# A hybrid pooling / state-space decoder step: another order for the first group of the scan

## The chip, the core and the metric

The kernel runs on one NeuronCore of a Trainium2 chip, in fp32. Five engines work from queues of their own, each strictly in order: TensorE (PE, matmuls and transposes into PSUM), VectorE (DVE), ScalarE (ACT), GpSimd (POOL) and SyncE (SP, which issues nearly all DMA loads and stores here). An instruction that waits for another engine or for a DMA holds up everything behind it in its queue. The metric is the device time of one execution in microseconds (us).

## The reference

One decoder layer for 512 prompt tokens and 8 sample rows (one new token each, with cached state), 520 columns in all. What matters here is the input projection and branch B, the state-space scan, in 8 groups of 4 heads:

```python
proj = h @ w_in                                # u | z | xBC | dt | gates
xbc  = causal_conv(xbc, prev, conv_w, conv_b)  # 4 taps, then silu; sample rows use their cached taps
dt   = softplus(dt_raw + dt_bias);  dA = dt * -exp(A_log)
Acs  = cumsum(dA within a chunk of 128)
decay  = exp(where(mask, Acs[l] - Acs[s], -inf))
scores = einsum(C, B)[..., None] * decay
y_diag = einsum(scores, x * dt)
h_next = h * exp(Acs[-1]) + einsum(B, exp(Acs[-1] - Acs), x * dt)
y_off  = einsum(C, h, exp(Acs))
y = (y_diag + y_off + D * x) * silu(z)         # then norm, projection, merge, FFN
```

Sample rows take one step of the same recurrence from a cached state: `h' = h * exp(dA) + dt * x * B`, `y = C . h'`.

## The kernel before

Activations lie transposed, channels on the 128 partitions and the 520 tokens along the row. A **unit** is a weight block of 128 output channels by 1024 inputs (512 KB): loaded by SP into `raw`, split into a high and a low part (`whi`, cast on ACT, L116; `wlo`, subtraction on DVE, L117), and used by one **column**, 48 matmuls of L129 (three products for each of 8 input blocks, two halves) into one of two PSUM buffers `m` (or into two banks). PE's order is the program order, in this part also that of ACT, DVE, POOL and, from `sp_order(True)` on, of SP: what is emitted first stands first in its engine's queue. `ahead(n)` emits load and split of units before they are due; `perform` keeps two units ahead.

Each group g of the scan has four convolution columns, x0, x1 (2 x 128 channels of x), bb and cc (B and C), and z columns zz. `conv` (L626) copies the PSUM result to `xb` and, scaled by the last tap, to `v` (ACT, L638, L639), and adds the other three taps (DVE, L646). POOL clears the 3 columns ahead of `xb` (L634), keeps the new conv state (`cvp`, `cvs`, L640, L641) and adds `cpre`, the cached taps of the sample rows, to the last 8 columns of `v` (L642). `end`, put off to the next `flush`, does tanh (ACT, L652), the product that completes silu (DVE, L653) and a copy of the 8 sample columns (POOL, L654) to `xs_s` or `bc_s`. `cpre` itself is made once by five POOL operations from the cached states `cvs` (L599 loads them, L604 and L606 multiply and add).

Columns of group 0 for dt, x0 and x1 are computed in `start`, while the norm is finished; its bb and cc columns are the first behind it. `dt_parts` makes dt and `acs` (DVE, some 17 small operations in `dtmp`) and stores `acs` to DRAM (`dacs`) and the sample rows' dt (`dds`, `dscr`), which come back spread over the partitions as `dtx`. `dec_load` brings `acs` back as `dec`, each row spread over all partitions (1 MB for a group; that of group 1 goes to a part of `aa`); the first `dec` lies where `dtmp` lay. `tokens_dt` transposes dt and `acs` on PE (L614) to `tok` (L616) inside the x1 column of group 1.

The rest comes in generators whose steps are strewn between columns. `decays` (L671): four chunks, each exp (ACT, L684, not for chunk 0), four Relu (L687) and exp (L688). `scan`: transposes of x and B (L717, L727), C.B (L734), masked to `cbm` (DVE, L736), chunk states (PE, L756), the chain of states `hst` (copy on ACT, L759; then three times a POOL product L761 and a DVE addition L763), `scores` (DVE, L742: `dec` times `cbm`), `decayed` (DVE, L695: `ce` times C) and two y (PE, L778, L780). `sample`, stepped by `part`: transpose of `bc_s` (PE, L806), a store and two loads (L809, L794, L795), the POOL product L799 and a DVE sum L803. For group 0 these steps stand among the columns of group 1.

Of the kernel before, what the change touches and what calls it, by code (L numbers as in the profile page):

```python
# [52 lines left out]
def tile_decoder(ctx: ExitStack, tc: tile.TileContext, I: dict, O: dict):  # L53
# [381 lines left out]
    def start():  # L435
# [88 lines left out]
        rest(4)  # L524
        ahead(2)
        for k in range(5, KD):
# [62 lines left out]
    def ssd_open(*_):  # L589
        G["yp_"], G["yp"] = opened("yp")  # L590
        G["ab_"], ab = opened("ab")
        G["aa"] = ab.tile([P, KD, T], F32, name="aa")
        S["pool"], S["sp"] = opened("ssd")
        sp = S["sp"]
        S["dt"] = dt_parts(sp)
        next(S["dt"])

        cvs = S["cvs"] = sp.tile([P, 32, NS, 4], F32, name="cvs")
        nc.sync.dma_start(out=cvs, in_=I["sconv"])  # L599
        cpre = sp.tile([P, 32, NS], F32, name="cpre")  # L600
        ctmp = sp.tile([P, 32, NS], F32, tag="gz", name="ctmp", bufs=2)
        for k in range(3):
            w = cwh[:, 32 * k : 32 * k + 32].unsqueeze(2).broadcast_to([P, 32, NS])
            nc.gpsimd.tensor_tensor(ctmp if k else cpre, cvs[:, :, :, k], w, ALU.mult)  # L604
            if k:
                nc.gpsimd.tensor_tensor(cpre, cpre, ctmp, ALU.add)  # L606
        S.update(cpre=cpre)
# [18 lines left out]
    def conv(i, outs, dst, keep, mix=None):  # L626
# [8 lines left out]
        with urgent():  # L635
            for o, t0, t1 in outs:
                shape = halves if t1 - t0 == T else lambda ap: ap
                nc.scalar.copy(shape(xb[:, 3 + t0 : 3 + t1]), o)  # L638
                nc.scalar.activation(shape(v[:, t0:t1]), o, AF.Identity, bias=cwh[:, 128 + i : 129 + i], scale=w(3))  # L639
        nc.gpsimd.tensor_copy(cvp[:, i], xb[:, TP : TP + 3])  # L640
        nc.gpsimd.tensor_copy(S["cvs"][:, i, :, 3], xb[:, TP + 3 : TP + 11])  # L641
        nc.gpsimd.tensor_tensor(v[:, TP:T], v[:, TP:T], S["cpre"][:, i], ALU.add)  # L642
        if mix:
            next(mix)
        for k in range(3):
            nc.vector.scalar_tensor_tensor(v[:, 0:TP], xb[:, k : k + TP], w(k), v[:, 0:TP], ALU.mult, ALU.add)  # L646
            if mix:
                next(mix)
        flush()

        def end():
            nc.scalar.activation(t, v, AF.Tanh, bias=0.0, scale=1.0)  # L652
            nc.vector.scalar_tensor_tensor(dst, t, 1.0, v, ALU.add, ALU.mult)  # L653
            nc.gpsimd.tensor_copy(keep, dst[:, TP:T])  # L654
# [44 lines left out]
    def scan(g, xg, bt, ct):  # L699
# [6 lines left out]
        tok = S["tok"]  # L706
        dec = S.pop(("dec", g))

# [55 lines left out]
        hst += hn  # L764
        scores((2, 3) if g else range(4))
        if not g:
            decayed(g, ct)
        nc.sync.dma_start(out=O["ssmp"][:, 256 * g : 256 * g + 256], in_=hst[4].rearrange("p h d -> p (h d)"))
        yield

        for i in range(2):
# [158 lines left out]
    def zend(i):  # L930
        return lambda: gated(i, S.pop(f"gz{i}"))

    def dt_more():
        next(S["dt"])

    for g in range(NG):
        todo(x0(g), *([X0(g)] if g else []))
        if g > 1:
            todo(step(g - 1))
        if g:  # L940
            todo(part(g - 1))
        todo(x1(g), *([X1(g)] if g else []))
        if g == 0:
            todo(dt_more)
        elif g == 1:
            todo(decay(0, 2))
            todo(step(0))
            todo(step(0))
        else:
            todo(step(g - 1))  # L950
# [4 lines left out]
        else:  # L955
            if g == 1:
                todo(decay(0, 2))
                todo(step(0))
            todo(part(g - 1))
            todo(decay(g))  # L960
        todo(cc(g), CC(g))
        if g:
            todo(part(g - 1))
            todo(decay(g))
            todo(zz(2 * g - 2), ZZ(2 * g - 2))
            todo(step(g - 1))
            todo(zend(2 * g - 2))
            todo(part(g - 1))
# [7 lines left out]
        if g:  # L976
            todo(part(g))
        else:
            todo(flush)
            todo(part(0))  # L980

# [575 lines left out]
```

## Time and profile before

| what | us |
|---|---|
| time, median of 3 runs (lowest to highest) | 1131.33 (1130.84 to 1132.9) |
| time of the profiled execution | 1131.08 |
| its span, first to last instruction | 1129.1 |
| PE busy in the span | 1078.7 (96%) |
| DVE, ACT, POOL busy | 697.6, 465.1, 349.2 |
| PE busy in 0 to 56, norm and first products | 47.4 |
| PE busy in 56 to 140, opening of the scan | 58.2 of 84 |
| PE busy in 140 to 500 | 359.7 of 360 |

PE is nearly always busy, so the few stretches in which it isn't are what an edit of the order can win, and the profile of such a stretch has to be read by what ended each wait. In a row of the timeline stand the start, the duration, the engine, the line, what is written and read, the count, and in brackets the idle time of the engine before it with what ended it. A list of waits gives the waiting instruction, the one that ended its wait, and total, count and longest in us. A row of the view by stretches ends with the granted PE clock (1.00 is full), the DMA engines' busy share, and GB/s.

### The profile page before, as it was taken

The page shows a single profiled execution, that of the slowest core. Times are in us where ns is not written, and L with a number is a line of the kernel's source. Part 1 is how long each engine was busy: PE and PEld are TensorE (multiplying, and loading weights), DVE is VectorE, ACT ScalarE, POOL GpSimd, SP SyncE. Part 2 cuts the span into 40 slices and gives each one's busy share as a digit, 9 for nine tenths or more (in the row PEclk, how much of TensorE's full clock was granted, in tenths as well). Part 3 has the DMA queues.
Part 4 walks back from the last instruction along what each step waited for, and adds up shares of the span by engine and source line. Part 5 has one row for each costly group of instructions (what it writes and reads, how often), then busy time and mean ns, then how long its engine had stood idle before and what let it go on. Part 6 is the DMA issues. An engine that isn't in the chain of part 4 may idle for free.

```text
span 1129.1 us, 22192 instructions
## 1 busy us (share of the span) xinstructions
PE 1078.7 (96%) x9345; PEld 1050.5 (93%) x9345; DVE 697.6 (62%) x963; ACT 465.1 (41%) x774; POOL 349.2 (31%) x498
## 2 busy tenths in 40 slices
PE   7949699999999999999999999999999999999995
PEld 6839599999999999999999999899999999999995
DVE  5663677787787788788757745655656653323332
ACT  4244646646656544575433323542222222222320
POOL 1131324334344342100000000289999960000001
PEclk9979799999999999999999999999999999999998
DMA  9326346246345332454435427356676652323212
GB/s 364 119 96 157 112 129 187 94 144 175 101 147 186 115 123 99 152 166 157 145 131 169 161 90 255 112 178 206 216 211 204 206 162 94 89 85 103 85 52 76
DMA packets 58467, 165.34 MB, mean 146 GB/s; under 512 B 10880, under 2 KB 16512, under 8 KB 57600
## 3 DMA queue, kind: packets, MB, share of 16 engines
q1 hardware_dynamic: 51712, 142.96, 39.0%
q0 software_dynamic: 6656, 20.98, 6.4%
q8 instruction: 73, 1.20, 0.4%
q14 instruction: 26, 0.21, 0.1%
HBM read 151.05 MB, written 12.86 MB: 145 GB/s over the span
## 4 chain that ended last, share of the span: by engine, by line
PE 88%; DVE 4%; issue 2%; DMA 2%; ACT 2%; POOL 1%; SPq 0%; DVEq 0%; POOLq 0%; ACTq 0%
PE m L129 77%; PE b L129 4%; PE b L778 2%; DMA raw<-in_win 1%; PE b L756 1%; PE b L780 1%; PE b L301 1%; DVE v L646 1%; PE b L734 1%; PE b L207 1%; PE b L717 1%; DVE acc L391 0%; DMA xT<-in_xT 0%; DMA raw<-in_wada 0%; POOL xn L1219 0%
## 5 line engine op out<-in xcount | busy, mean ns | idle before, releaser
L129 PE MATMUL m<-hh,whi 128*128 128x260 f32 (+1 forms) x1840 | 382.0, 287 | 1.7 <-ACT hh L475 1.0
L129 PE MATMUL m<-hl,whi 128*128 128x260 f32 (+1 forms) x1840 | 375.2, 284 | 3.3 <-DVE hl L481 3.1
L129 PE MATMUL m<-hh,wlo 128*128 128x260 f32 (+1 forms) x1840 | 375.2, 284 | 0.0
L117 DVE TENSOR_TENSOR wlo<-raw,whi 128x1024 fp32r<-128x1024 f32 (+2 forms) x169 | 234.0, 1387 | 151.1 <-ACT whi L116 148.3
L116 ACT CAST whi<-raw 128x1024 fp32r<-128x1024 f32 (+2 forms) x169 | 173.1, 1027 | 357.4 <-PE m L129 240.2
L129 PEld LDWEIGHTS m<-hh,whi 128*128 128x128 f32 x1840 | 287.1, 190 | 8.0 <-issue 3.2
L129 PEld LDWEIGHTS m<-hl,whi 128*128 128x128 f32 x1840 | 286.3, 190 | 4.1 <-DVE hl L481 3.8
L129 PEld LDWEIGHTS m<-hh,wlo 128*128 128x128 f32 x1840 | 286.9, 190 | 0.0
L341 POOL TENSOR_TENSOR r<-me,mhalf 128x5 f32<-128x5 f32 (+2 forms) x6 | 6.4, 1065 | 439.9 <-DVE me L340 439.9
L646 DVE SCALAR_TENSOR_TENSOR v<-xb,cwh,v 128x512 f32<-128x512 f32 x96 | 72.9, 760 | 52.8 <-ACT v L639 30.2
L1323 DVE TENSOR_TENSOR fs<-m,fs 128x520 f32<-128x520 f32 (+2 forms) x23 | 15.4, 675 | 70.6 <-PE m L129 69.8
L638 ACT COPY xb<-m 128x520 f32<-128x520 f32 (+1 forms) x31 | 17.9, 577 | 93.4 <-PE m L129 93.4
L129 PE MATMUL m<-ah,whi 128*128 128x260 f32 x264 | 53.2, 283 | 0.0
L129 PE MATMUL m<-ah,wlo 128*128 128x260 f32 x264 | 53.1, 282 | 0.0
L129 PE MATMUL m<-al,whi 128*128 128x260 f32 x264 | 53.0, 282 | 0.0
L129 PE MATMUL m<-gh,whi 128*128 128x260 f32 x256 | 52.8, 288 | 0.0
L129 PE MATMUL m<-gl,whi 128*128 128x260 f32 x256 | 51.3, 282 | 0.0
L129 PE MATMUL m<-gh,wlo 128*128 128x260 f32 x256 | 51.3, 282 | 0.0
L1312 POOL TENSOR_TENSOR hs<-hs,ht 128x512 f32<-128x512 f32 x32 | 47.8, 1494 | 0.8
L799 POOL TENSOR_TENSOR h<-h,cc 128x1024 f32<-128x1024 f32 x16 | 38.3, 2395 | 25.2 <-DMA cc<-dbc 24.2
L1310 POOL TENSOR_TENSOR ht<-bb,xds 128x512 f32<-128x512 f32 x32 | 41.0, 1282 | 2.2 <-DMA bb<-dbc 1.7
L129 PEld LDWEIGHTS m<-gh,whi 128*128 128x128 f32 x256 | 39.2, 188 | 2.5 <-PE b L301 1.3
(300 smaller groups left out, 1747.3 us busy)
## 6 DMA issues: line engine op xcount, KB each, us to landing
raw<-in_win SPq DMA_DIRECT2D x73, 512.0 KB, 4.8
raw<-in_wfi SPq DMA_DIRECT2D x44, 512.0 KB, 4.4
araw<-in_wada SPq DMA_DIRECT2D x24, 512.0 KB, 4.2
h<-in_sssm SPq DMA_DIRECT2D x16, 512.0 KB, 4.1
raw<-in_wssd SPq DMA_DIRECT2D x16, 512.0 KB, 3.4
hs<-in_sssm POOLq DMA_DIRECT2D x32, 256.0 KB, 4.1
out_ssms<-hs POOLq DMA_DIRECT2D x32, 256.0 KB, 3.5
raw<-in_wfo SPq DMA_DIRECT2D x16, 512.0 KB, 3.5
```

Source lines behind the costliest of these rows:

```text
L116: nc.scalar.copy(hi, raw)
L117: nc.vector.tensor_tensor(lo, raw, hi.bitcast(F32), ALU.subtract)
L129: nc.tensor.matmul(o, a[:, k, c0 : c0 + P], b[:, t0:t1], start=f, stop=e)
L207: nc.tensor.matmul(ps[32 * i : 32 * i + 32, 0:n], sc[:, k], raw[:, n * i : n * i + n], start=first, stop=last)
L301: nc.tensor.matmul(ps[32 * i : 32 * i + 32, 0:256], scr[:, k], w[:, 256 * i : 256 * i + 256], start=k == 0 and j == 0, stop=k == KD - 1 an ...
L638: nc.scalar.copy(shape(xb[:, 3 + t0 : 3 + t1]), o)
L646: nc.vector.scalar_tensor_tensor(v[:, 0:TP], xb[:, k : k + TP], w(k), v[:, 0:TP], ALU.mult, ALU.add)
L778: nc.tensor.matmul(o, xdt[:, c, 2 * i + h], dec[:, c, 2 * i + h], start=c == 0, stop=False)
L799: nc.gpsimd.tensor_tensor(h0, h0, cc.unsqueeze(2).broadcast_to([P, 4, 2, P]), ALU.mult)
L1310: nc.gpsimd.tensor_tensor(t, bb.unsqueeze(2).broadcast_to([P, 2, 2, P]), at(xds), ALU.mult)
L1312: nc.gpsimd.tensor_tensor(h, h, t, ALU.add)
L1323: nc.vector.tensor_tensor(view(s[:, t0:t1]), u, view(s[:, t0:t1]), ALU.mult)
```

## The change

Six edits, all in the order of emission. (1) `ahead(3)`: a third unit (x0 of group 1) is loaded and split ahead of the end of `start`. (2) The making of `cpre` becomes `conv_state`, called in the x1 convolution of group 0 behind its taps instead of in `ssd_open`. (3) The three small POOL operations of `conv` (add of `cpre`, `cvp`, `cvs`) move from behind the ACT operations into `end`, ahead of tanh, for all 32 convolutions. (4) The decay chunks of group 0 (`decay(0)`) and the first of group 1 are emitted later, and the scores and `ce` products of group 0 one step later than the end of the state chain, with an added `yield`. (5) The first sample steps (`part(0)`) come later, the transpose of `bc_s` behind the x1 column of group 1, and the others follow. (6) `dec` of a group is kept in `S` rather than popped.

```diff
@@ -522,7 +522,7 @@
         rows(5, 6)
         products(4)
         rest(4)
-        ahead(2)
+        ahead(3)
         for k in range(5, KD):
             products(k)
         first["ps"] = outs
@@ -597,6 +597,10 @@
 
         cvs = S["cvs"] = sp.tile([P, 32, NS, 4], F32, name="cvs")
         nc.sync.dma_start(out=cvs, in_=I["sconv"])
+
+    def conv_state():
+
+        sp, cvs = S["sp"], S["cvs"]
         cpre = sp.tile([P, 32, NS], F32, name="cpre")
         ctmp = sp.tile([P, 32, NS], F32, tag="gz", name="ctmp", bufs=2)
         for k in range(3):
@@ -637,18 +641,20 @@
                 shape = halves if t1 - t0 == T else lambda ap: ap
                 nc.scalar.copy(shape(xb[:, 3 + t0 : 3 + t1]), o)
                 nc.scalar.activation(shape(v[:, t0:t1]), o, AF.Identity, bias=cwh[:, 128 + i : 129 + i], scale=w(3))
-        nc.gpsimd.tensor_copy(cvp[:, i], xb[:, TP : TP + 3])
-        nc.gpsimd.tensor_copy(S["cvs"][:, i, :, 3], xb[:, TP + 3 : TP + 11])
-        nc.gpsimd.tensor_tensor(v[:, TP:T], v[:, TP:T], S["cpre"][:, i], ALU.add)
         if mix:
             next(mix)
         for k in range(3):
             nc.vector.scalar_tensor_tensor(v[:, 0:TP], xb[:, k : k + TP], w(k), v[:, 0:TP], ALU.mult, ALU.add)
             if mix:
                 next(mix)
+        if i == 1:
+            conv_state()
         flush()
 
         def end():
+            nc.gpsimd.tensor_tensor(v[:, TP:T], v[:, TP:T], S["cpre"][:, i], ALU.add)
+            nc.gpsimd.tensor_copy(cvp[:, i], xb[:, TP : TP + 3])
+            nc.gpsimd.tensor_copy(S["cvs"][:, i, :, 3], xb[:, TP + 3 : TP + 11])
             nc.scalar.activation(t, v, AF.Tanh, bias=0.0, scale=1.0)
             nc.vector.scalar_tensor_tensor(dst, t, 1.0, v, ALU.add, ALU.mult)
             nc.gpsimd.tensor_copy(keep, dst[:, TP:T])
@@ -704,7 +710,7 @@
             decayed(g, ct)
         yield
         tok = S["tok"]
-        dec = S.pop(("dec", g))
+        dec = S["dec", g]
 
         xdt = sp.tile([P, 4, 4, 64], F32, tag="xdt", name=f"xdt{g}")
         xde = sp.tile([P, 4, 4, 64], F32, tag="xde", name=f"xde{g}")
@@ -762,11 +768,14 @@
             yield
             nc.vector.tensor_tensor(hn[c], hn[c], sv[c], ALU.add)
         hst += hn
-        scores((2, 3) if g else range(4))
-        if not g:
-            decayed(g, ct)
+        if g:
+            scores((2, 3))
         nc.sync.dma_start(out=O["ssmp"][:, 256 * g : 256 * g + 256], in_=hst[4].rearrange("p h d -> p (h d)"))
         yield
+        if not g:
+            scores(range(4))
+            decayed(g, ct)
+            yield
 
         for i in range(2):
             yb = bank()
@@ -930,6 +939,9 @@
     def zend(i):
         return lambda: gated(i, S.pop(f"gz{i}"))
 
+    def scores_first():
+        next(gens[0])
+
     def dt_more():
         next(S["dt"])
 
@@ -937,15 +949,17 @@
         todo(x0(g), *([X0(g)] if g else []))
         if g > 1:
             todo(step(g - 1))
-        if g:
+        if g == 2:
+            todo(part(0))
+        if g > 1:
             todo(part(g - 1))
         todo(x1(g), *([X1(g)] if g else []))
         if g == 0:
             todo(dt_more)
         elif g == 1:
-            todo(decay(0, 2))
             todo(step(0))
             todo(step(0))
+            todo(part(0))
         else:
             todo(step(g - 1))
         todo(bb(g), BB(g))
@@ -954,16 +968,22 @@
             todo(dt_more)
         else:
             if g == 1:
-                todo(decay(0, 2))
                 todo(step(0))
+                todo(decay(0, 3))
+            else:
+                todo(decay(g))
             todo(part(g - 1))
-            todo(decay(g))
         todo(cc(g), CC(g))
+        if g == 1:
+            todo(decay(0))
+            todo(scores_first)
         if g:
             todo(part(g - 1))
             todo(decay(g))
             todo(zz(2 * g - 2), ZZ(2 * g - 2))
             todo(step(g - 1))
+            if g == 1:
+                todo(decay(1))
             todo(zend(2 * g - 2))
             todo(part(g - 1))
             todo(decay(g))
@@ -977,7 +997,6 @@
             todo(part(g))
         else:
             todo(flush)
-            todo(part(0))
 
     todo(sp_order(False))
     todo(lambda: ordered.__exit__(None, None, None) and None)
```

**PE and POOL, opening.** PE's queue around the sample transpose, before: `m51` is the cc column of group 0, `m55` the x0 column of group 1.

```order
L129 MATMUL m51_800<-hl_102,whi42_564 128x260 x2
L129 MATMUL m51_800<-hh_101,wlo42_565 128x260 x2
L806 MATMUL b52_870<-cst_75,bc_s_91 16x128
L129 MATMUL m55_882<-hh_101,whi46_772 128x260 x2
L129 MATMUL m55_882<-hl_102,whi46_772 128x260 x2
```

PE's queue around the same transpose after the change (now L815): `m57` is the x1 column of group 1, `m65` its bb column.

```order
L129 MATMUL m57_941<-hh_101,wlo49_791 128x260 x2
L723 MATMUL b59_1014<-cst_75,xg0_652 128x128 x4
L723 MATMUL b60_1021<-cst_75,xg0_652 128x128 x4
L733 MATMUL b61_1028<-cst_75,bt0_705 128x128 x4
L815 MATMUL b62_1034<-cst_75,bc_s_91 16x128
L129 MATMUL m65_1046<-hh_101,whi52_870 128x260 x2
```

The transpose has gone behind two columns and the transposes of x and B. POOL's queue at the same place of the program, before:

```order
L604 TENSOR_TENSOR cpre_646<-cvs_644,cwh_96 128x256
L604 TENSOR_TENSOR ctmp_647<-cvs_644,cwh_96 128x256
L606 TENSOR_TENSOR cpre_646<-cpre_646,ctmp_647 128x256
L604 TENSOR_TENSOR ctmp_647<-cvs_644,cwh_96 128x256
L606 TENSOR_TENSOR cpre_646<-cpre_646,ctmp_647 128x256
L634 MEMSET xb0_654 128x3
L640 COPY cvp_89<-xb0_654 128x3
L641 COPY cvs_644<-xb0_654 128x8
L642 TENSOR_TENSOR v0_655<-v0_655,cpre_646 128x8
```

and POOL after the change:

```order
L638 MEMSET xb0_653 128x3
L638 MEMSET xb1_664 128x3
L608 TENSOR_TENSOR cpre_675<-cvs_650,cwh_96 128x256
L608 TENSOR_TENSOR ctmp_676<-cvs_650,cwh_96 128x256
L610 TENSOR_TENSOR cpre_675<-cpre_675,ctmp_676 128x256
L608 TENSOR_TENSOR ctmp_676<-cvs_650,cwh_96 128x256
L610 TENSOR_TENSOR cpre_675<-cpre_675,ctmp_676 128x256
L655 TENSOR_TENSOR v0_654<-v0_654,cpre_675 128x8
L656 COPY cvp_89<-xb0_653 128x3
```

The two memsets now stand ahead of the five operations, which are still ahead of everything else.

**SP, the loads of the opening.** SP's queue before, from the store of `acs` on (`raw50` is the cc unit of group 1, `raw54` and `raw57` its two z units, `aa` the decays of group 1):

```order
L575 DMA dacs_782<-acs_700 128x128
L581 DMA dscr_787<-dds_784 32x2x8
L585 DMA dtx_93<-dscr_787 64x16x8 x4
L107 DMA raw50_797<-in_win 128x1024
L668 DMA dec0_864<-dacs_782 128x4x512
L668 DMA aa_629<-dacs_782 128x4x512
L809 DMA dbc_97<-bcs0_872 16x128
L107 DMA raw54_879<-in_win 128x1024
L794 DMA h0_0_0_943<-in_sssm 128x1024
L795 DMA cc_0_0_944<-dbc_97 128x512
L107 DMA raw57_951<-in_win 128x1024
```

SP after the change (`raw53` and `raw56` are the z units now):

```order
L107 DMA raw50_794<-in_win 128x1024
L674 DMA dec0_861<-dacs_779 128x4x512
L674 DMA aa_635<-dacs_779 128x4x512
L107 DMA raw53_874<-in_win 128x1024
L107 DMA raw56_939<-in_win 128x1024
L818 DMA dbc_97<-bcs0_1036 16x128
L107 DMA raw64_1043<-in_win 128x1024
L803 DMA h0_0_0_1136<-in_sssm 128x1024
L804 DMA cc_0_0_1137<-dbc_97 128x512
```

The sample rows' store and loads have gone behind both z units and the next x0 unit.

**ACT and POOL, the state chain of group 0.** ACT's queue around the copy that opens the chain, before (`t17` is the tanh of group 1's bb; `aa` and `ce1` belong to the decays of group 1):

```order
L116 CAST whi67_1158<-raw57_951 128x1024
L638 COPY xb25_1214<-m69_1165 128x520
L639 ACTIVATE v25_1215<-m69_1165,cwh_96 128x520
L759 COPY hst0_0_1229<-b70_1223 128x256
L652 ACTIVATE t17_1117<-v17_1116 128x520
L684 ACTIVATE ce1_1152<-aa_629 128x512
```

ACT after the change; here the last three rows are the fourth decay chunk of group 0:

```order
L116 CAST whi67_1140<-raw56_939 128x1024
L642 COPY xb25_1196<-m69_1147 128x520
L643 ACTIVATE v25_1197<-m69_1147,cwh_96 128x520
L765 COPY hst0_0_1208<-b70_1202 128x256
L658 ACTIVATE t17_1097<-v17_1096 128x520
L690 ACTIVATE aa_635<-dec0_861 128x512
L693 ACTIVATE dec0_861<-dec0_861,tok_964 128x128 x4
L694 ACTIVATE dec0_861<-dec0_861 128x512
```

POOL's queue there, before:

```order
L640 COPY cvp_89<-xb17_1115 128x3
L641 COPY cvs_644<-xb17_1115 128x8
L642 TENSOR_TENSOR v17_1116<-v17_1116,cpre_646 128x8
L654 COPY xs_s_90<-xg1_881 128x8
L799 TENSOR_TENSOR h0_0_0_943<-h0_0_0_943,cc_0_0_944 128x1024
L634 MEMSET xb25_1214 128x3
L640 COPY cvp_89<-xb25_1214 128x3
L641 COPY cvs_644<-xb25_1214 128x8
L642 TENSOR_TENSOR v25_1215<-v25_1215,cpre_646 128x8
L761 TENSOR_TENSOR hst0_1_1230<-hst0_0_1229,cd0_1023 128x256
L761 TENSOR_TENSOR hst0_2_1231<-hst0_1_1230,cd0_1023 128x256
L761 TENSOR_TENSOR hst0_3_1232<-hst0_2_1231,cd0_1023 128x256
```

and after the change:

```order
L638 MEMSET xb25_1196 128x3
L767 TENSOR_TENSOR hst0_1_1209<-hst0_0_1208,cd0_1117 128x256
L767 TENSOR_TENSOR hst0_2_1210<-hst0_1_1209,cd0_1117 128x256
L767 TENSOR_TENSOR hst0_3_1211<-hst0_2_1210,cd0_1117 128x256
L655 TENSOR_TENSOR v17_1096<-v17_1096,cpre_675 128x8
L656 COPY cvp_89<-xb17_1095 128x3
L657 COPY cvs_650<-xb17_1095 128x8
L660 COPY bc_s_91<-bt1_1045 128x8
L808 TENSOR_TENSOR h0_0_0_1136<-h0_0_0_1136,cc_0_0_1137 128x1024
```

The add to `v17`, which its tanh needs, and the sample product have gone from ahead of the state chain to behind it; the `bt` copy stands between them.

## The prediction, as made before the result was known

> **What bounds the kernel now.** I read the list of what TensorE (PE) waited for first, then its timeline. From 60 to 140 us the list names two waits: the one in the first timeline row below (16.94 us, ended by POOL), and this one (total, times, longest). None of that size follows.
>
> ```profile
> PE b L778 <- DVE dec L742: 8.9, 1, 8.9
> ```
>
> ```profile
> 83.40 0.38 PE L806 MATMUL b<-cst,bc_s 128*16 128x128 f32 x1 [16.94 <-POOL xb L634]
> ...
> 98.73 0.49 PE L129 MATMUL m<-hh,whi 128*128 128x260 f32 x2
> ...
> 132.00 0.80 PE L129 MATMUL m<-hh,whi 128*128 128x260 f32 x2
> ```
>
> The first hole is the sample transpose L806: it stands in PE's queue ahead of the x0 column of group 1 and needs `bc_s`, the end of all four first convolutions. The second is y of group 0 (L778), which needs the masked decays. Three times matter below: the start of the first hole (83.40 less 16.94 is 66.46), the bb column of group 1 at 98.73, and the zz1 column behind both holes at 132.00. After 132.00 PE is the bound again, so **the change is worth what it moves that zz1 column**, as long as later groups do not lose it again.
>
> **The opening: sample rows' preparation later.** Before, the five `cpre` operations (L604, L606) stand in POOL's queue ahead of the memset of `xb`, and DVE's six convolution steps wait for them.
>
> ```profile
> 59.17 0.75 POOL L604 TENSOR_TENSOR cpre<-cvs,cwh 128x256 f32<-128x256 f32 x1 [18.21 <-issue]
> ```
> ```profile
> 63.15 4.58 DVE L646 SCALAR_TENSOR_TENSOR v<-xb,cwh,v 128x512 f32<-128x512 f32 x6 [5.90 <-POOL xb L634]
> ```
>
> Now the memset is first, so DVE may begin at about 59.2, when ScalarE (ACT) has written `v`, and 3.9 us seem won. But `cpre` starts at 59.17 all the same (it waits only for the load of `cvs`), and it must still end before tanh, since the add of `cpre` now stands ahead of it. What do the two engines do side by side?
>
> ```profile
> 122.87 0.61 POOL L761 TENSOR_TENSOR hst<-hst,cd 128x256 f32<-128x256 f32 x1
> 124.01 1.05 POOL L761 TENSOR_TENSOR hst<-hst,cd 128x256 f32<-128x256 f32 x1 [0.53 <-DVE hst L763]
> 125.60 1.05 POOL L761 TENSOR_TENSOR hst<-hst,cd 128x256 f32<-128x256 f32 x1 [0.53 <-DVE hst L763]
> ```
> ```profile
> 123.85 0.74 DVE L646 SCALAR_TENSOR_TENSOR v<-xb,cwh,v 128x512 f32<-128x512 f32 x1
> ```
>
> The same POOL operation takes 0.61 alone and 1.05 when it meets that DVE step; 123.85 + 0.74 + 0.61 = 125.2 against a real end of 125.06. They take turns. So six steps (4.58) and five `cpre` (3.9) need 8.5 us from 59.17 on: 67.7, where they ended before. Bounds: 0.7 later (all DVE first, then `cpre`, add and tanh) to 3.9 earlier (no turns); I take 0, by the row. [...]
>
> **Three units split ahead, transpose moved.** The third weight split leaves the middle of the opening: one cast on ACT and one subtraction (1.22) on DVE. Its place is now ahead of `dt`, where DVE stands idle for 3.3 us until PE has ended the first products and ACT has read them:
>
> ```profile
> 56.95 0.30 DVE L553 SCALAR_TENSOR_TENSOR dtmp<-dtmp 128x136 f32<-128x136 f32 x1 [3.34 <-ACT dtmp L552]
> ```
>
> So it costs nothing there; without that cover it would move `dt` and all behind it by up to the 1.2 us of this row:
>
> ```profile
> 76.98 1.22 DVE L117 TENSOR_TENSOR wlo<-raw,whi 128x1024 fp32r<-128x1024 f32 x1
> ```
> ```profile
> 77.10 0.78 ACT L639 ACTIVATE v<-m,cwh 128x520 f32<-128x520 f32 x1 [0.91 <-DVE xg L653]
> ```
>
> PE now runs the x0 column of group 1 from 66.5 to 72.2 (a column is 5.76, row below). The x1 column needs the PSUM buffer of the cc column, which that ACT row frees at 77.9. So the 16.9 us hole becomes one of **5.6**. PE restarts at half clock after it (0.50, third number from the end in the stretch 85:86 below), which costs some 2 us of the x1 column and nothing of the path, because of what comes next.
>
> ```profile
> 141.64 5.76 PE m L129 x48
> ```
>
> PE must then wait for the token copy. `tok` on ACT stands behind the split of the CC unit, whose 512 KB load is issued by SyncE (SP) behind four `dtx` loads:
>
> ```profile
> 83.87 1.08 SPq L107 DMA_DIRECT2D raw<-in_win  x1
> 93.86 0.38 SPq L668 DMA_DIRECT2D dec<-dacs  x1
> ...
> 97.03 1.61 SPq L794 DMA_DIRECT2D h<-in_sssm  x1
> ```
> ```profile
> 85.00:86.00 1.00, 1.00 (x7) 1.00 (x6) 0.95 (x1) 0.02 (x1) 0.00 (x0) 0.50 0.40 23
> ...
> 88.00:89.00 1.00, 1.00 (x10) 1.00 (x10) 0.00 (x0) 0.00 (x0) 0.00 (x0) 0.93 0.47 180
> ...
> 94.00:95.00 1.00, 1.00 (x11) 1.00 (x10) 0.96 (x2) 0.48 (x1) 0.00 (x0) 1.00 0.08 12
> ```
> ```profile
> 94.08 0.48 ACT L616 COPY tok<-b 128x384 f32<-128x384 f32 x1 [0.27 <-PE b L614]
> ```
>
> The stretches' last two numbers are the DMA engines' busy share and GB/s: that load ended at about 88.6. Without the 1.2 us subtraction ahead of `dds`, SP runs 1.1 earlier: 87.5. Plus 1.0 for the cast and 0.48 for `tok`, PE starts its bb column at 89.2 instead of 98.73: **9.5 us earlier**. If that were the whole path, this would be the gain.
>
> **Decays and DMA order.** It is not the whole path. The `dec` load shares its tile with `dtmp`, so SP held it until PE had transposed the tokens:
>
> ```profile
> SPq L668 <- PE b L614: 9.0, 1, 9.0
> ```
>
> Now the tokens are through at about 82, and `dec` goes out as soon as SP is free of the CC unit, at 83.9: 10 us earlier. The next weights (ZZ 0) come right behind `dec` and `aa`, 1 MB each. In the run before they landed at 110.04, where ACT waited for them:
>
> ```profile
> 110.04 1.05 ACT L116 CAST whi<-raw 128x1024 fp32r<-128x1024 f32 x1 [2.60 <-DMA raw<-in_win]
> ...
> 112.16 0.63 ACT L652 ACTIVATE t<-v 128x520 f32<-128x520 f32 x1
> 112.68 0.63 ACT L684 ACTIVATE aa<-dec 128x512 f32<-128x512 f32 x1
> ...
> 115.20 0.62 ACT L684 ACTIVATE aa<-dec 128x512 f32<-128x512 f32 x1
> ...
> 121.89 0.37 ACT L759 COPY hst<-b 128x256 f32<-128x256 f32 x1
> ```
>
> That is 15.1 after `dec`'s first bytes (94.95). In the changed kernel those first bytes move at 85.0 if the queue lets them (1.1 after issue, as before), or at 87.5 if they stand wholly behind `dtx` and the CC load. So ZZ 0 lands between 100.1 and 102.6. With the DMA engines busy for 40% of 85:86, more than half of their time is free there: I take the middle, **101.4, that is 8.6 us earlier**. [...]
>
> ACT stands still in front of that cast (from about 91 on), because the decays now come behind it. From the cast to the copy of `hst` it has the same work: the group 1 chunk ahead of the copy (2.1) gives way to `cd` and the first chunk of group 0 (2.1). So the copy starts 11.85 later, at 113.25, and the `hst` chain, then the first score, would follow 8.6 earlier.
>
> ```profile
> 127.02 2.49 DVE L742 TENSOR_TENSOR dec<-dec,cbm 128x512 f32<-128x512 f32 x4
> ```
> ```profile
> 115.52 2.40 POOL L799 TENSOR_TENSOR h<-h,cc 128x1024 f32<-128x1024 f32 x1
> ```
>
> Two **new waits** take part of it. The tanh of group 1's bb (`t17`) now needs the POOL add of `cpre`, which stands behind all three `hst` operations; the last of these ends at 118.05 (125.60 + 1.05 before, less 8.6). Behind `t17` in ACT's queue stands the fourth decay chunk of group 0. So: about 0.2 for the add, `t17` (0.6) to 118.85, a chunk (2.5, from 112.68 to 115.20): ready at 121.35. DVE does `bt` and the first score (0.6 each, a quarter of the 2.49), to 120.1, and then waits. Into that hole comes the sample product (2.40, the row above), next in POOL's queue after `bt`, and it holds the turn until 122.55; DVE's second score begins there, against 127.64 before (127.02 and a quarter of 2.49). That is 5.1 earlier; 0.25, an estimate, goes to short POOL operations among the three scores and three products of `ce` that remain ahead of y. **Sum: 4.8 us**. The price of the sample product is between 0 (it lands late: second score 121.35, sum 6.0) and 1.2, which I take.
>
> The profiled execution took 1131.08 (span 1129.1); less 4.8 is 1126.3. The median is 0.25 above it, so 1126.5.
>
> **Rivals.**
> (1) *More is won*: the DMA queue passes `dec` at once (1.3), the sample product misses the hole (1.2), or `cpre` and the DVE steps overlap (up to 3.9, which moves SP and all behind it). For: 85:86 is far from full. Against: the 1.05 row. All three: 6.4 more, 1120; one or two: 1122 to 1125.
> (2) *The load is hidden less*: ZZ 0 shares the queue with the ZZ 1 unit behind it, as the earlier one did with `h`, which landed late:
> ```profile
> DMA to landing us min/median/max: 3.1/7.2/15.3
> ```
> `h` landed at 97.03 + 15.3 = 112.3, 17.4 after the first bytes. With 87.5 + 17.4 ZZ 0 comes at 104.9: 3.5 worse, 1130.0. Against: the earlier one landed 2.3 before `h`.
> (3) *Slower*: in every later group tanh of x1 also waits on POOL behind the `hst` chain, and ACT stands still for some 4.6 us there (in group 0 the chain ran from the copy's end, 122.26, to 126.65, and the add comes after it).
> ```profile
> 165.25 1.03 ACT L116 CAST whi<-raw 128x1024 fp32r<-128x1024 f32 x1
> ```
> ```profile
> 175.99 0.51 PE L129 MATMUL m<-hh,whi 128*128 128x260 f32 x2
> ```
> This split, 1.03 on ACT and 1.22 on DVE, would be ready at 165.25 + 4.6 + 2.3 = 172.2; PE uses it at 176.0. Some 3.8 us of slack remain. From 3.8 us of further delay on, PE waits in each of six groups; 1.2 us beyond that point is 7 us, 1133.7. Against: nothing I see adds 3.8.
> (4) *The change doesn't do what it says*: PE still stands at the x0 column of group 1, because the third split or its load comes late. Then nothing moves: 1131. Against: the load is now issued ahead of `cvs`, and the split has until 66.
>
> **How the numbers follow.** Forecast, 1124.8 to 1128.5: 0.45. (1): 0.23. (2): 0.20. (3): 0.08. (4): 0.04. A measurement of this kernel tells about 0.2% (2.3 us) from no change, so faster ends at 1129.07: forecast, (1) and a fifth of (2), 0.72. Within 0.2%: the rest of (2), (4), 0.19. Slower: (3) and a little, 0.09. The range takes in the forecast, most of (1) and (2): 1121 to 1131; the ends of all open costs together (1120, 1133.7) are left out.
>
> **What the changed profile would show.** PE's wait at L806 gone, one of 5 to 6 us at the x1 column of group 1, bb column near 89; `dec` issued near 84; ACT waiting some 10 us for the ZZ 0 load, its cast near 101; PE's wait at y of group 0 not shorter but longer, about 11 us; zz1 column near 127. No new PE waits after 140. I am wrong if ZZ 0 lands after 104 or before 99, if DVE's first steps end well before 67, or if PE waits return in later groups.

## The result, and the profile after

| | median of | lowest to highest, us | ratio to before, 95% interval |
|---|---|---|---|
| before, in the same runs | 1131.35 us, 5 | 1130.84 to 1133.69 | |
| changed | 1125.30 us, 5 | 1120.82 to 1125.95 | 0.993, 0.9907 to 0.9954 |
| changed, a second set (`again` below) | 1124.11 us, 6 | 1123.57 to 1126.49 | 0.9928, 0.9913 to 0.9943 |

The changed kernel is faster by 0.5 to 0.9%. Its profiled execution took 1125.83 us (span 1124.1). These are all the waits of PE from 60 to 140 us in it (what waited, for what: total, times, longest):

```profile
PE b L787 <- ACT dec L693: 8.4, 1, 8.4
PE b L815 <- ACT tok L620: 4.6, 1, 4.6
PE m L129 <- ACT v L643: 3.5, 1, 3.5
PE b L787 <- DVE dec L748: 2.2, 1, 2.2
```

They add to 18.7 us, against 25.8 before (16.9 and 8.9). The hole at the sample transpose is down to 4.6 us and is now ended by `tok`, no longer by the fourth convolution; a new one of 3.5 us stands at the x1 column, where the forecast had one of 5.6; and the wait at y of group 0 (L787) has grown from 8.9 to 10.6 us in two pieces. PE's timeline has the same, with start, length and the wait ahead in brackets; the last row is the zz1 column, on which the prediction set its sum:

```profile
90.55 0.37 PE L815 MATMUL b<-cst,bc_s 128*16 128x128 f32 x1 [4.61 <-ACT tok L620]
...
120.48 0.69 PE L787 MATMUL b<-dec,xdt 128*64 128x128 f32 x4 [8.37 <-ACT dec L693]
...
123.34 1.91 PE L787 MATMUL b<-dec,xdt 128*64 128x128 f32 x12 [2.17 <-DVE dec L748]
...
126.97 0.80 PE L129 MATMUL m<-hh,whi 128*128 128x260 f32 x2
```

The zz1 column starts at 126.97 instead of 132.00. ACT's timeline shows what leads there: the ZZ 0 cast after a wait of 9.05 us for its load, the copy of `hst`, and tanh of bb held up by POOL:

```profile
101.76 1.05 ACT L116 CAST whi<-raw 128x1024 fp32r<-128x1024 f32 x1 [9.05 <-DMA raw<-in_win]
...
113.61 0.37 ACT L765 COPY hst<-b 128x256 f32<-128x256 f32 x1
118.41 0.64 ACT L658 ACTIVATE t<-v 128x520 f32<-128x520 f32 x1 [4.43 <-POOL v L655]
```

One more row is needed from SP, the issue of `dec`:

```profile
84.25 0.49 SPq L674 DMA_DIRECT2D dec<-dacs  x1
```

With it the whole difference can be split by landmarks. From before to after `dec` is issued 9.61 us earlier (93.86 to 84.25). From there to the ZZ 0 cast it takes 17.51 us instead of 16.18, and from the cast to the zz1 column 25.21 instead of 21.96. So 9.61 - 1.33 - 3.25 = 5.03 us, which is what the zz1 column gained; the profiled time fell by 5.25.

### The profile page after: what moved, and what is told of

Its sections match the earlier page's. It is cut to its first block, busy times and chain, and to the rows that moved or that the text cites. A ratio compares the mean times of both kernels' runs of the same rounds, so it can differ in the third digit from the quotient of the medians.

```text
span 1124.1 us, 22173 instructions
## 1 busy us (share of the span) xinstructions
PE 1081.5 (96%) x9345; PEld 1052.6 (94%) x9345; DVE 700.8 (62%) x963; ACT 463.4 (41%) x774; POOL 349.0 (31%) x498
## 4 chain that ended last, share of the span: by engine, by line
PE 88%; DVE 3%; DMA 2%; issue 2%; ACT 2%; POOL 1%; SPq 0%; POOLq 0%; DVEq 0%; ACTq 0%
PE m L129 77%; PE b L129 4%; PE b L787 2%; DMA raw<-in_win 1%; PE b L762 1%; PE b L789 1%; PE b L301 1%; PE b L207 1%; DVE v L647 1%; PE b L740 1%; PE b L723 1%; DMA xT<-in_xT 0%; ACT whi L116 0%; DMA raw<-in_wada 0%; POOL xn L1238 0%
## 5 line engine op out<-in xcount | busy, mean ns | idle before, releaser
L1329 POOL TENSOR_TENSOR ht<-bb,xds 128x512 f32<-128x512 f32 x32 | 46.7, 1460 | 2.2 <-DMA bb<-dbc 1.7
L1331 POOL TENSOR_TENSOR hs<-hs,ht 128x512 f32<-128x512 f32 x32 | 43.9, 1372 | 0.8
```

Source lines behind the costliest of these rows:

```text
L1329: nc.gpsimd.tensor_tensor(t, bb.unsqueeze(2).broadcast_to([P, 2, 2, P]), at(xds), ALU.mult)
L1331: nc.gpsimd.tensor_tensor(h, h, t, ALU.add)
```

## The experiments

All are edits of the changed kernel. Times are medians with the number of executions; ratios are to the kernel before, run beside them: its median was 1132.52 us beside again, warm24, open_early and ahead2, 1132.02 beside dec_first, aa_late, adds_ahead and product_late, and 1131.38 beside the last four to be run, so the ratios compare better than the medians. The landmarks come from the profile of each: when the last input of `start` is cast (last row of L475), when SP issues `dec`, when the ZZ 0 cast begins, when the zz1 column begins.

| kernel | last L475 | dec issued | ZZ 0 cast | zz1 | dec after start | cast after dec | zz1 after cast | median, us |
|---|---|---|---|---|---|---|---|---|
| before | 49.64 | 93.86 | 110.04 | 132.00 | 44.22 | 16.18 | 21.96 | 1131.35 |
| changed | 52.20 | 84.25 | 101.76 | 126.97 | 32.05 | 17.51 | 25.21 | 1125.30 (5) |
| again | 49.23 | 81.28 | 99.74 | 124.95 | 32.05 | 18.46 | 25.21 | 1124.11 (6) |
| warm24 | 48.12 | 80.66 | 100.87 | 126.08 | 32.54 | 20.21 | 25.21 | 1123.64 (6) |
| open_early | 52.09 | 86.22 | 104.64 | 129.84 | 34.13 | 18.42 | 25.20 | 1124.94 (6) |
| ahead2 | 50.51 | 87.34 | 105.99 | 131.21 | 36.83 | 18.65 | 25.22 | 1126.84 (6) |
| sample_back | 52.34 | 93.64 | 111.04 | 136.25 | 41.30 | 17.40 | 25.21 | 1132.10 (12) |
| sample_back_own | 52.73 | 84.83 | 103.53 | 129.28 | 32.10 | 18.70 | 25.75 | 1124.46 (6) |
| dec_first | 49.38 | 81.47 | 99.99 | 119.83 | 32.09 | 18.52 | 19.84 | 1117.60 (4) |
| aa_late | 52.31 | 84.38 | 96.56 | 122.46 | 32.07 | 12.18 | 25.90 | 1118.38 (4) |
| adds_ahead | 52.40 | 84.49 | 102.62 | 127.51 | 32.09 | 18.13 | 24.89 | 1124.14 (6) |
| product_late | 49.27 | 81.28 | 99.77 | 123.95 | 32.01 | 18.49 | 24.18 | 1120.78 (5) |
| adds_product | 52.28 | 84.50 | 102.92 | 125.64 | 32.22 | 18.42 | 22.72 | 1119.73 (4) |
| all4 | 49.02 | 81.20 | 99.13 | 116.69 | 32.18 | 17.93 | 17.56 | 1113.49 (4) |

A reader can use it like a ledger: each edit should move one column of differences and leave the others. The cast stands for the landing of ZZ 0, for which it waits, in all rows but that of all4, where it stands behind three decay chunks and finds the load there.

### Does the change make the start late? (again, warm24)

In the first profile `start` ended 2.56 us later than before the change, ahead of anything that the change touches on PE. Windows of 4 us show what went with it: each row has the window, its length, the busy time of PE, its weight loads, DVE, ACT and POOL, and behind these PE's granted clock, the DMA engines' busy share and GB/s. Before, changed, warm24:

```profile
14.00:18.00 4.00, 3.64 (x48) 3.29 (x48) 1.68 (x5) 1.30 (x2) 1.17 (x1) 1.00 1.05 436
```
```profile
14.00:18.00 4.00, 3.83 (x39) 3.09 (x38) 1.39 (x2) 1.17 (x2) 1.17 (x1) 0.64 1.04 432
```
```profile
14.00:18.00 4.00, 3.64 (x48) 3.29 (x48) 1.77 (x5) 1.30 (x2) 1.17 (x1) 1.00 1.04 431
```

```diff
-WARM = 17, 7
+WARM = 24, 7
```

> The changed kernel unaltered, a second time, to see how far its executions differ. In its first profile the end of `start` (last cast of L475) came at 52.20 us against 49.64 in the profile of before, and PE's first adaLN products (L207, 14.64 us) took 3.19 instead of 1.94 us at a granted clock of 0.64. Theory A, the late start is a matter of the execution (where PE's warm-up and its 2.67 us pause fall in the clock's steps) and not of the change: executions of the changed kernel fall in two bunches some 2.5 to 4 us apart, near 1121 and near 1125.5; when this profile shows 1.94 us at L207 its total is near 1121. Theory B, the change (the third load and split) makes it: every profile of the changed kernel has the last L475 at 52 us, and the times stay at 1122.5 to 1126.

> The changed kernel with 24 instead of 17 products in PE's first warm-up, which fills 1.9 of the 2.67 us that PE stands idle ahead of the sums of L330; nothing else differs. Theory A (the granted clock at 14 us decides, and an idle PE loses it): L207 takes 1.94 us, the last cast of L475 is at 49.7, the time near 1121 to 1122 in all executions. Theory B (the change makes the late start): no effect, 1125.3.

**Measured.** The unaltered kernel's second profile has `start` ending at 49.23, with a clock of 1.00 at 14 to 18 us: the same program does both. Of all profiles in the table, the seven that end it at 52.0 us or later have a clock of 0.63 to 0.71 in 14:18 and of 0.66 to 0.74 in 24:28; a low clock in one of these windows alone goes with an end at 49.02 (all4, 0.71 in the first), 50.51 (ahead2, 0.50 in the first) or 49.27 (product_late, 0.65 in the second). So the late start is a matter of the execution, not of the change; how often it comes before the change, one profile can't tell. What lowers the clock these profiles do not show; the length of PE's pause alone does not. Ahead of L330, just before the window 14:18, PE paused 2.67 us in the first profile (clock 0.64 in that window), 2.24 before the change and 2.06 in `again` (1.00 in both), but 1.45 in ahead2 (0.50); and behind the pause of 3.48 us at the x1 column of the first profile the clock was 1.00 (79:80). The times did not fall in two clear bunches as theory A had it: they spread from 1120.8 to 1126.5, and the execution with the early start took 1123.85, not 1121. With 24 products the clock was 1.00 from 10 to 18 and from 24 to 44 us and `start` ended at 48.12, but the time hardly moved (1123.64; ratio 0.9916, 0.9899 to 0.9933): in its profile ZZ 0 came 20.21 us after the issue of `dec`, so the load gave back what the start had won. `dec` and `aa` took 10.7 and 16.9 us to land there, near the 10.4 and 16.6 of `again`; but ZZ 0 landed 2.8 us behind `aa` rather than 1.3. Why is open.

### What the opening and the third split are worth (open_early, ahead2)

```diff
         nc.sync.dma_start(out=cvs, in_=I["sconv"])
+        conv_state()
...
-        if i == 1:
-            conv_state()
         flush()
```

> The changed kernel with the five preparing operations of the sample rows (`cpre`) put back ahead of the memset of `xb` in POOL's queue. The prediction (DVE's convolution step and POOL's product take turns, so the place of `cpre` is worth 0): from the start of the first `cpre` operation to the scan that makes `acs` it takes as long as in the changed kernel, 12.9 us, and the time stays within 0.5 us. The rival (they overlap in part: 1.07 us a pair where turns would take 1.47): that stretch grows by 1.7 to 14.6 us as before the change, `dec` is issued 1.7 later and the time rises by 1.7, less what the later ZZ 0 load hides.

**Measured.** Changed kernel, POOL and DVE in the opening:

```profile
61.24 0.76 POOL L608 TENSOR_TENSOR cpre<-cvs,cwh 128x256 f32<-128x256 f32 x1 [3.50 <-DMA cvs<-in_sconv]
61.95 1.24 POOL L608 TENSOR_TENSOR ctmp<-cvs,cwh 128x256 f32<-128x256 f32 x1
63.27 1.07 POOL L610 TENSOR_TENSOR cpre<-cpre,ctmp 128x256 f32<-128x256 f32 x1
64.42 1.08 POOL L608 TENSOR_TENSOR ctmp<-cvs,cwh 128x256 f32<-128x256 f32 x1
```
```profile
61.84 6.14 DVE L647 SCALAR_TENSOR_TENSOR v<-xb,cwh,v 128x512 f32<-128x512 f32 x6 [2.03 <-ACT v L643]
```

With `cpre` back in front, the same operations one after the other:

```profile
61.52 0.75 POOL L609 TENSOR_TENSOR cpre<-cvs,cwh 128x256 f32<-128x256 f32 x1 [18.13 <-DMA cvs<-in_sconv]
...
63.06 0.74 POOL L611 TENSOR_TENSOR cpre<-cpre,ctmp 128x256 f32<-128x256 f32 x1
```
```profile
65.51 4.57 DVE L648 SCALAR_TENSOR_TENSOR v<-xb,cwh,v 128x512 f32<-128x512 f32 x6 [5.82 <-POOL xb L639]
```

Side by side a POOL operation starts every 1.15 us (64.42 - 63.27) while DVE does one step; in turns it would be 0.74 + 0.76 = 1.50. From the first `cpre` (61.24) to the end of DVE's six steps it takes 6.74 us, not the 8.56 of open_early (61.52 to 70.08). So the edit wins 1.8 us there and 2.08 by the issue of `dec` (34.13 against 32.05 after the start): **the prediction's 0 was wrong**. PE's hole at the x1 column, 3.5 us in the changed kernel, is 5.6 us here, which is the size that the prediction had worked out with its 0:

```profile
80.30 0.80 PE L129 MATMUL m<-hh,whi 128*128 128x260 f32 x2 [5.62 <-ACT v L644]
```

The medians are too coarse for 2 us here (ratio 0.9937, 0.9922 to 0.9952, beside 0.9928 for `again`); the trace carries this verdict.

```diff
-        ahead(3)
+        ahead(2)
```

> The changed kernel with two units split ahead instead of three. The prediction (the third split lies free in DVE's wait ahead of `dt`, and costs 1.2 us ahead of `dds` where it stood before): `dds` and all that SP issues behind it come 1.1 us later, ZZ 0 lands 1.1 later, time up by 1.1. Theory B of the late start (the third load makes it): `start` ends 2.5 us earlier and the time falls by 1.4. Rival: the split was hidden where it stood, no difference (under 0.5).

**Measured.** 1126.84 us (ratio 0.9949, 0.9932 to 0.9966), and `dec` is issued 4.8 us later after the start, not 1.1. On PE the x0 column of group 1 stands:

```profile
77.29 0.80 PE L129 MATMUL m<-hh,wlo 128*128 128x260 f32 x2 [6.34 <-DVE wlo L117]
```

Its low part is subtracted only after the `dt` operations (PE had waited 2.9 us more for the high part just ahead of that), so the hole that the moved transpose had vacated comes back under another name, the x1 column and the tokens in it slip, and `dec` waits for them. The third split is what lets PE use that hole; the 1.2 us of DVE time are the small part. That DVE time is free in its new place: in the changed kernel the wait ahead of `dt` is 2.19 us instead of 3.34, and `dt` begins at 59.50, 7.30 us behind the last L475, as before (56.95, 7.31).

```profile
59.50 0.30 DVE L553 SCALAR_TENSOR_TENSOR dtmp<-dtmp 128x136 f32<-128x136 f32 x1 [2.19 <-ACT dtmp L552]
```

The late start was no effect of the third load either: `start` ends at 49.23 with it in `again`, and at 50.51 without it here.

### Is PE's hole the loss, or what it holds back? (sample_back, sample_back_own)

```diff
             todo(flush)
+            todo(part(0))
...
             todo(step(0))
             todo(step(0))
-            todo(part(0))
```

sample_back_own adds this, so that the `dec` tile no longer waits for the readers of `dtmp`:

```diff
-        tmps = sp.tile([P, 9, 136], F32, tag="dec", name="dtmp")
+        tmps = G["aa"][:, 0:3].rearrange("p a b -> p (a b)")[:, 0:1224].rearrange("p (a b) -> p a b", a=9)
```

> The changed kernel with the first step of group 0's sample (its transpose and store) put back ahead of the x0 column of group 1. The prediction (PE stands at it until the fourth convolution is through; the tokens inside the x1 column and with them the release of `dec` come late): PE waits 14 to 17 us at L815 again, the tokens are transposed near 91, `dec` is issued near 92 instead of 81 to 84, ZZ 0 lands 17.5 to 18.5 behind it at 109 to 111, the zz1 column comes at 132 to 134: 1130 to 1132. Rival (the gain came from the opening and the third split, and the hole was slack): `dec` and ZZ 0 stay within 2 us, 1124 to 1127.

> As sample_back, but with `dtmp` in a part of `aa` that is free then, so that `dec` need not wait for the transposes of the tokens. Theory (PE's hole is not worth its length, it costs through the late issue of `dec` alone): PE's wait at L815 stays at 14 to 17 us, yet `dec` is issued at 81 to 85, ZZ 0 lands within 1.5 us of where it does in the changed kernel, PE's waits at y of group 0 shrink from 11 to some 5 to 9, and the time is that of the changed kernel, 1124 to 1126. Rival (PE's hole itself carries the gain): as sample_back, 1130 or more, at best 1128.

**Measured.** sample_back, on PE, SP and ACT:

```profile
83.88 0.38 PE L815 MATMUL b<-cst,bc_s 128*16 128x128 f32 x1 [14.72 <-POOL xb L638]
```
```profile
93.64 0.38 SPq L674 DMA_DIRECT2D dec<-dacs  x1
```
```profile
111.04 1.04 ACT L116 CAST whi<-raw 128x1024 fp32r<-128x1024 f32 x1 [11.30 <-DMA raw<-in_win]
```

sample_back_own, the same:

```profile
84.36 0.38 PE L815 MATMUL b<-cst,bc_s 128*16 128x128 f32 x1 [14.81 <-POOL xb L638]
...
122.78 0.70 PE L787 MATMUL b<-dec,xdt 128*64 128x128 f32 x4 [3.72 <-ACT dec L693]
```
```profile
84.83 0.54 SPq L674 DMA_DIRECT2D dec<-dacs  x1
```
```profile
103.53 1.05 ACT L116 CAST whi<-raw 128x1024 fp32r<-128x1024 f32 x1 [3.36 <-DMA raw<-in_win]
```

This pair is the clearest of the study. (The zz1 column of sample_back comes later than the 132 to 134 expected, at 136.25, in a profile with the late start.) With the transpose back in front the whole gain is gone (ratio to before 1.0005, 0.9993 to 1.0016; 12 executions). With the same 14.8 us hole on PE but `dec` free of it, the gain is there (0.9941, 0.9929 to 0.9953), though not all of it by the landmarks: from the end of `start` to the zz1 column it takes 76.55 us, against 74.77 and 75.72 in the two profiles of the changed kernel and 82.36 before. So PE's time in the first hole was hardly a loss by itself: the second hole, at y, swallowed it (8.4 us of wait there become 3.7). The hole cost what it held back, the transposes of the tokens, and through them the release of `dec` and all loads behind it.

### What sets the second hole (dec_first, aa_late)

dec_first puts three decay chunks of group 0 ahead of the bb column, and so ahead of the ZZ 0 cast in ACT's queue; aa_late issues group 1's `dec` (in `aa`) behind the ZZ units.

```diff
             todo(part(0))
+            todo(decay(0, 3))
...
                 todo(step(0))
-                todo(decay(0, 3))
```
```diff
-            dec_load(g + 1)
+            if g:
+                dec_load(g + 1)
...
         elif g == 1:
+            todo(lambda: dec_load(1))
             todo(step(0))
```

> The changed kernel with the first three decay chunks of group 0 emitted ahead of the bb column of group 1, and so ahead of the ZZ 0 cast on ACT, which stood idle for 9.05 us before that cast. Theory (the ZZ 0 load holds up the decays only because the cast stands ahead of them in ACT's queue; `dec` itself lands some 6 us before ZZ 0): three chunks run from about 95 on, the copy of `hst` comes at 107 instead of 113.6, the zz1 column 5 to 6.7 us earlier, time 1118 to 1120. Rival (`dec` shares the DMA queues with ZZ 0 and lands only at 100 or later): the cast slips behind the chunks to 107 to 109, PE waits 3 to 5 us at the ZZ 0 column, and nothing is gained, 1124 to 1126.

> The changed kernel with the load of group 1's decays (`aa`, 1 MB) issued behind the ZZ 0 and ZZ 1 units instead of ahead of them. Theory (ZZ 0 lands 17.5 us after `dec` is issued because 2 MB of spread rows stand ahead of it): it lands 3 to 7 us earlier, the cast at 95 to 98.5, the waits of PE at y of group 0 (10.6 us together) shrink by as much, the zz1 column and the time by 3 to 6: 1119 to 1122. Rival (the DMA engines serve all queued loads side by side, the order on SP matters little): the cast stays within 1 us, 1125.

**Measured.** dec_first, ACT and PE:

```profile
91.84 0.23 ACT L682 ACTIVATE cd<-dec 128x16 f32<-128x16 f32 x1 [1.95 <-DMA dec<-dacs]
...
99.99 1.05 ACT L116 CAST whi<-raw 128x1024 fp32r<-128x1024 f32 x1 [0.95 <-DMA raw<-in_win]
```
```profile
113.28 0.70 PE L787 MATMUL b<-dec,xdt 128*64 128x128 f32 x4 [3.87 <-DVE dec L748]
```

aa_late:

```profile
96.56 1.05 ACT L116 CAST whi<-raw 128x1024 fp32r<-128x1024 f32 x1 [3.66 <-DMA raw<-in_win]
```
```profile
115.97 0.69 PE L787 MATMUL b<-dec,xdt 128*64 128x128 f32 x4 [3.68 <-ACT dec L693]
```

Both do what the theory said, and the times lie 0.4 and 0.6 us below the ranges given. `dec` had landed at 91.84, 8 us ahead of ZZ 0; ACT's in-order queue alone kept the decays behind the cast. And ZZ 0 comes 12.18 us after the issue of `dec` where `aa` is not ahead of it, against 17.4 to 20.2 in the other profiles of the changed order (all4 apart, where the cast did not wait for it) and 16.18 before: its 1 MB costs 5.3 us against the changed kernel. Ratios 0.9872 (0.9855 to 0.9890) and 0.9876 (0.9858 to 0.9895), so either edit alone brings a further 0.5%, where the whole change brought 0.7%. dec_first also says something of the change itself: before it, two chunks stood in just this place, ahead of the bb column, and its fourth edit moved them behind. With `dec` early, the old place is the better one: with three chunks in it, dec_first takes 5.4 us from between the cast and the zz1 column (25.21 to 19.84).

### The two new waits (adds_ahead, product_late, adds_product)

```diff
+        if i > 1:
+            keeps()
         if mix:
             next(mix)
...
         def end():
-            nc.gpsimd.tensor_tensor(v[:, TP:T], v[:, TP:T], S["cpre"][:, i], ALU.add)
...
+            if i < 2:
+                keeps()
```

(`keeps` holds the three POOL operations.) product_late moves one step of the sample:

```diff
         if g:
-            todo(part(g - 1))
+            if g > 1:
+                todo(part(g - 1))
...
             if g == 1:
+                todo(part(0))
                 todo(decay(1))
```

> The changed kernel with POOL's three small operations of a convolution (add of `cpre`, two copies) back ahead of DVE's steps, and so ahead of the `hst` chain, for all columns but x0 and x1 of group 0. [...] Rival (product and score overlap in part, as `cpre` and the convolution steps did): scores end 1.7 us earlier, 1123 to 1123.5. If the wait in later groups costs anything, more.

> The changed kernel with the sample product of group 0 (POOL, 2.35 us) moved behind the last score, after the z gate's copy. [...] Rival (the scores wait for their decays anyway): no difference.

> The edits of adds_ahead and product_late together, on the changed kernel. Alone, the first moved the scores by nothing (the fourth chunk was ready, the sample product took the time back) and the second by 1.0 us. Theory (the two waits cover each other): together the four scores run without a gap right behind the `hst` chain, 2.5 us in all, and end 1.5 to 2.5 us earlier than in the changed kernel against the ZZ 0 cast (22.7 us behind the start of that cast there); time 1.5 to 2.5 below the changed kernel, 1122 to 1123. Rival (the edits add): 1.0, the same as product_late alone.

**Measured.** The scores of group 0 on DVE with the product on POOL. Changed kernel:

```profile
119.69 0.68 DVE L748 TENSOR_TENSOR dec<-dec,cbm 128x512 f32<-128x512 f32 x1
121.57 2.93 DVE L748 TENSOR_TENSOR dec<-dec,cbm 128x512 f32<-128x512 f32 x3 [1.19 <-ACT dec L694]
```
```profile
120.38 2.35 POOL L808 TENSOR_TENSOR h<-h,cc 128x1024 f32<-128x1024 f32 x1
```

adds_ahead:

```profile
120.37 4.65 DVE L754 TENSOR_TENSOR dec<-dec,cbm 128x512 f32<-128x512 f32 x4
```
```profile
121.07 2.80 POOL L814 TENSOR_TENSOR h<-h,cc 128x1024 f32<-128x1024 f32 x1
```

product_late, and adds_product:

```profile
119.57 1.90 DVE L748 TENSOR_TENSOR dec<-dec,cbm 128x512 f32<-128x512 f32 x3 [1.19 <-ACT dec L694]
```
```profile
120.67 2.49 DVE L754 TENSOR_TENSOR dec<-dec,cbm 128x512 f32<-128x512 f32 x4
```

Against the product three scores take 2.93 us instead of 1.90, while the product keeps its 2.35: here DVE does wait, 1.03 us. With the adds early, DVE has no wait for the fourth chunk, but four scores take 4.65 instead of 2.49, 2.2 us more, beside a product that now lies wholly within them (2.80 from 121.07 on): from cast to zz1 the edit is worth 0.32 us, the product's removal 1.03, both 2.49. **The two waits cover each other**, as the prediction's chain had it. The time of adds_ahead is that of the changed kernel (ratio 0.9930, 0.9911 to 0.9949). Those of the other two fell further than their traces explain (0.9899, 0.9882 to 0.9917; 0.9892, 0.9876 to 0.9909), by the ratios 3.3 and 4.1 us more than `again`; with 5 and 4 executions these differences are known to some 2.5 us, so that 1.03 and 2.49 lie inside. From the zz1 column to the end it took 997.3 and 997.9 us in these two profiles, 998.9 in those of the changed kernel; over the whole table it is 996.5 (all4) to 999.9 (adds_ahead), and nothing here explains these differences.

### All four together (all4)

> The edits of dec_first, aa_late, adds_ahead and product_late together. Theory (one hole of PE ahead of y of group 0, 6.1 us in the profile of dec_first, with three things in a row at its end): ACT no longer waits for ZZ 0 behind the decay chunks (0.95), the product no longer meets the scores (1.0), the fourth chunk is ready when the chain ends (1.5): 2.5 to 3.5 below dec_first, 1114 to 1115.5. If decays and load order added up in full it would be 1108 to 1110. Rival (the chain of `hst` is what remains and moves with nothing): 1116.5 to 1118.

**Measured.** 1113.49 us (1112.78 to 1115.53, 4 executions), ratio 0.9847, 0.9832 to 0.9861: the fastest kernel here, 1.5% below before. PE at y of group 0:

```profile
112.46 2.50 PE L793 MATMUL b<-dec,xdt 128*64 128x128 f32 x16 [3.24 <-DVE dec L754]
```

The hole is 3.2 us, down from 10.6. The time lies 0.5 us below the range that was expected. The edits do not add up in full, as expected: decay order and load order shorten the same hole, and once the decays run at 92 us the `hst` chain and four scores end it. With 24 warm-up products beside it, it was not run.

Taken back alone, the edits of the change thus weigh very differently: the moved transpose carries the gain (sample_back), because it frees `dec`; the third split is worth 4.8 us and the later `cpre` 2.1 by the issue of `dec`; the POOL operations moved behind the chain are worth nothing (adds_ahead, all but two columns), and the decays would have done better ahead of the bb column, by 5.4 us (dec_first). These amounts do not add up.

## Why the prediction came out, point by point

The forecast was 1126.5 us; the two sets gave 1125.30 and 1124.11, the first inside its own 1124.8 to 1128.5, the second a little below.

- **The opening, taken at 0: wrong.** It is worth 2.1 us by the issue of `dec`. The step that failed is the reading of one row (a POOL product of 1.05 us beside one DVE step) as a rule for all pairs: turns hold for the score against the sample product (1.03 us lost), not for `cpre` against the convolution steps (1.15 us a pair, not 1.50). In the profiled execution a start 2.56 us later hid the miss by luck, so that `dec` at 84.25 looks like the forecast's 83.9 and the zz1 column at 126.97 like its 127.2. In `again`, with the start as before, `dec` is issued at 81.28 and the zz1 column comes at 124.95; DVE's first steps end at 65.0 there, which is the prediction's own sign of being wrong ("well before 67"). That this term is also what put both medians below the forecast is likely, not shown. It was part of rival 1.
- **The third split, free where it went: right** (`dt` begins 7.30 us behind the last L475, 7.31 before). That its old place would do more harm than 1.2 us was not seen (4.8, ahead2).
- **A hole at the x1 column, 5.6: mechanism right, 3.5 measured.** The 2.1 us of the opening are the difference: with them taken back, in open_early, the hole is 5.6. The clock behind the 3.5 was 1.00 (79:80), not the 0.50 of the forecast.
- **The bb column 9.5 us earlier, but not the path: right.** It came at 90.6 and 87.7 (forecast 89.2), and sample_back_own shows that PE's time there was worth little by itself.
- **`dec` released early, ZZ 0 17.5 us behind it: right.** 17.51 in the profiled execution and 18.46 in `again`; aa_late shows that what is ahead in SP's queue sets it. Against 16.18 before, it is `dec` and `aa` that land late, as the prediction had it for loads behind the CC unit: 9.8 and 15.7 us after their issue (10.4 and 16.6 in `again`), where it was 8.4 and 14.5 before, and 8.3 and 14.4 in sample_back, where the CC unit was through. Rival 2 (ZZ 0 shares its queue with ZZ 1, some 3.5 us later) did not come: ZZ 0 lands 1.3 us behind `aa` in both profiles, as before. In warm24, ahead2 and sample_back it is 2.6 to 2.9, and why is open.
- **Two new waits: right, to a few tenths.** From the cast to the `hst` copy 11.85 us forecast and measured; tanh of bb through at 118.85 forecast, 119.05 measured; PE's waits at y 11 forecast, 10.6 measured; from cast to zz1 25.8 forecast, 25.21 measured.
- **Rival 3, waits in later groups: did not come.** Behind 140 us PE has no new wait. **Rival 4** fell with the first rows: PE has no wait left at the x0 column.

## What to carry to other kernels

Price a stall by what is queued behind it, not by its length: 14.8 us of an idle PE cost next to nothing once the load that stood behind it was set free, and 5 us hung on a single 1 MB load in the wrong place of a DMA queue. Where a chain ends in several waits in a row, removing one shows little until the next goes too; the ledger of landmarks (issue, landing, first use) tells which stretch an edit moved when medians cannot. Whether two engines hold each other up has to be measured for the pair of operations at hand. And an order chosen for one set of landing times has to be looked at again when an edit moves them: once `dec` came early, the decays did better ahead of the bb column.

## What was not expected of the hardware

- VectorE and GpSimd do not always take turns: 1.15 us for a pair of 0.76 and 0.74 (convolution step and `cpre`), but the scores lost 1.03 of the 1.16 us that were left of a 2.35 us product when they were ready.
- The granted clock in the first 45 us differs between executions of one program (1.00 or 0.64 at 14 to 18 us), and the end of a 50 us stage differs with it by 3 us; with seven more warm-up products, which fill PE's pause, it was 1.00 there in the one profile taken.
- A load of 512 KB issued behind 2 MB of spread rows landed 16.2 to 20.2 us after the first of them was issued, behind 1 MB after 12.2 us.
